# The first half's mixers as steps between the in-projections' products, in place of a ranked plan, with their loads and stores on GpSimd's queue

## The chip, the core and the metric

The kernel runs on one core of one Trainium2 chip. The metric is device time in microseconds of one execution; less is better. A core has five engines with queues of their own, each worked off strictly in order: PE (TensorE, matrix products), DVE (VectorE), ACT (ScalarE), POOL (GpSimd) and SP (SyncE, used here only to issue transfers). Transfers run on 16 DMA engines.

## The reference, cut to what matters

One hybrid decoder layer on x of 2048 tokens by 1024 features, in fp32. Three mixers read one common projection z and feed one common output projection, and an MLP follows:

```
h = rmsnorm(x, norm1_g)
z = einsum("bsd,dc->bsc", h, w_in)          # q,k,v (384 each) | conv a,gate (256 each) | gate,x (384 each)
y_attn = attention_mixer(q, k, v)           # 6 heads in 3 dilated windows, ALiBi
y_conv = silu(layernorm(conv31(a * sigmoid(gate))))
y_lru  = gelu(gate) * rg_lru(conv4(x))      # a scan along the sequence
x = x + concat(y_attn, y_conv, y_lru) @ w_out
x = x + square(relu(rmsnorm(x, norm2_g) @ w_up)) @ w_down
return rmsnorm(x, final_g)
```

## The kernel before, in words

**Tiles.** Everything lies transposed, 128 features on the partitions and tokens along the free axis. The sequence is worked in two halves h = 0, 1 of 1024 tokens. Each fp32 operand is split into two parts (`split`, L242 to L246: ACT rounds the value, DVE takes the difference), and each product is three matmuls (`products`, L262, L265, L268). The weights of a group come through `load_w` (L251 load on SP's queue, L242 on ACT, L243 on DVE), with five landing tiles (`raw`) and four pairs of split weights (`rounded6` and its neighbours), so that loads and splits run at most a few products ahead of PE.

**In-projection.** `inproj(h)` (L324) takes the groups of z's columns in the order of `COLUMN_ORDER`. For h = 0 these are [11, 9, 12] together, then [10], [0], [3], V, [1], [4], [2], [5], [16], [13], [17], [14], and [18, 15] together; for h = 1 all stand alone but the last pair, and V comes late. A one-tile group holds two PSUM banks of 512 tokens and 8 rounds of products: 48 matmuls of 128x512. `evac` (L390, L393) multiplies the finished banks by the norm's factor on DVE, and stores z to DRAM. V (`project_v`, L410) is computed with the tokens on the partitions: twice 4 banks, each time 8 weight tiles of 128x384 and 96 matmuls, 192 in all; DVE splits the 16 weight tiles (L243) and empties the 8 banks (L433). There are four main banks, so V uses all of them. Ahead of h = 1 stand its activations: 16 loads of `xt`, split on ACT (L245) and DVE (L246) with the sum of squares (L276, L277), and after its first group the norm (L286, L287 on PE, L361 on ACT, two reciprocals L362 on DVE).

**Mixers.** `mixers(0)` is a chain of generator steps: attention, then the 31-tap convolution (62 operations of 128x1024 on DVE, L472 and L474) with its layer norm, then the LRU (three tiles: a load of `lscr`, 4 taps L557 and L561, gate products L573 to L575 with ACT's sigmoids, a scan on DVE L591), then `combine` of attention. `conv_ahead(HS)` computes 31 of the second half's taps. Each `yield` names the step's cost on DVE in us.

**What sets the order.** The program is recorded in the order of the code, and a list scheduler then orders each engine's queue. In this kernel `inproj(0)` is recorded whole; ACT is told to issue two DRAM-to-DRAM copies of 4 MB each (`out_w`, `down_w`) behind its last instruction of `inproj(0)`; `setup()` (LRU gate weights and zeros, 17 small loads and stores) is placed behind the last load of x. Then `mixers(0)` is recorded as one block at a low rank (`high_priority(offset=-1500)`), and `conv_ahead(HS)` likewise inside `inproj(1)`: the scheduler fits their instructions into both in-projections wherever its ranking finds room. The first half's convolution, LRU and `combine` load and store on SP's queue, attention loads on POOL's. The second half's mixers already run in another manner, by `tick`:

```
    def tick(share):
        chore()
        credit[0] = min(credit[0] + share, 2.0 * share)
        if aside[0] is None or credit[0] <= 0:
            return
        ...
        cost = next(aside[0], None)
        ...
            credit[0] -= cost
```

Each call adds a share of credit and records at most one step, which is then bound to stand behind the products recorded so far on PE, DVE and ACT.

Of the kernel before, what the change touches and what calls it, by code (L numbers as in the profile page):

```python
# [15 lines left out]
HS = 1024  # L16
# [23 lines left out]
OUT_SHARE, UP_SHARE, DOWN_SHARE = 0.7, 1.0, 1.0  # L40
# [39 lines left out]
def body(tc, xt, w_in, w_v, w_out, w_up, w_down, vecs, lru_wa, lru_wx, consts, g_row, out, out_rows):  # L80
# [45 lines left out]
    def z_tile():  # L126
        return zp.tile([P, HS], F32, name="z", tag="Z")
# [175 lines left out]
    def project(src, group, acts, nk, evac, hook=None):  # L303
        banks = [[main_bank() if i < 2 else mix_bank() for _ in range(2)] for i in range(len(group))]
        w = {}
        if not len(acts):
            acts.between = lambda: w.update({0: load_w(src(group[0], 0))})
        for k in range(nk):
            while len(acts) < k + 1:
                acts.more()  # L310
            if hook is not None and k == hook[0]:
                hook[1]()
            for i, t in enumerate(group):
                if k % 4 == 0 and (k or i not in w):
                    w[i] = load_w(src(t, k // 4))
                products(banks[i], w[i], k % 4, acts[k], k == 0, k == nk - 1)
            while len(acts) < (min(k + 2, nk) if k < 4 else nk):
                acts.more()
        for i, t in enumerate(group):
            evac(t, banks[i])  # L320
# [3 lines left out]
    def inproj(h, after=None):  # L324
# [44 lines left out]
        def evac(t, banks):  # L369
            z = z_tile()  # L370
            for b, bank in enumerate(banks):
# [37 lines left out]
        def project_v():  # L409
# [8 lines left out]
            for c0 in range(0, HS // P, 4):  # L418
                banks = [main_bank()[:, :VW] for _ in range(4)]
                for k in range(KT):  # L420
                    wh, wl = load_w(w_v[k])
                    ah, al = acts[k]
                    for i, bank in enumerate(banks):
                        c = slice((c0 + i) * P, (c0 + i + 1) * P)
                        nc.tensor.matmul(bank, ah[:, c], wh, start=k == 0, stop=False)
                        nc.tensor.matmul(bank, ah[:, c], wl, start=False, stop=False)
                        nc.tensor.matmul(bank, al[:, c], wh, start=False, stop=k == KT - 1)
                for i, bank in enumerate(banks):
# [7 lines left out]
        for n, grp in enumerate(cols_):  # L436
            if grp[0] < 0:
                project_v()
                continue
            if after is not None:  # L440
                after(n)
# [11 lines left out]
    def loads(h):  # L453
        return nc.gpsimd if h else nc.sync

    def stores(h):
        return nc.gpsimd if h else nc.sync

    def conv_taps(t0, n, early, tiles=(0, 1)):
# [6 lines left out]
        yield 0  # L466
        yield 0
# [11 lines left out]
    def conv_norm(t0, yc, early):  # L479
        tile_, q = wide_tile if early else mtile, nc.sync if early else nc.gpsimd  # L480
# [39 lines left out]
    def conv_ahead(t0):  # L520
        a, = yield from conv_taps(t0, HS, True, (0,))
        nc.sync.dma_start(cscr, a)
# [13 lines left out]
    def lru_mixer(h):  # L536
# [6 lines left out]
        for t0 in range(h * HS, (h + 1) * HS, n):  # L543
            for t in range(3):
# [9 lines left out]
                if h:  # L554
                    yield 0
                    yield 0
# [7 lines left out]
                for c in range(0, n, NB):  # L564
# [3 lines left out]
                    yield 0  # L568
# [90 lines left out]
    def attention(h):  # L659
# [18 lines left out]
        yield 0  # L678
        yield 0
# [50 lines left out]
        for n, (g, bt, half) in enumerate(sets):  # L730
            for uu in range(2):
# [35 lines left out]
                if uu == 0 and n + 1 < len(sets):  # L767
                    got = fetch_keys(h, *sets[n + 1])
# [105 lines left out]
    def mixers(h):  # L874
# [5 lines left out]
        else:  # L880
            yield from attention(0)
            yield from conv_whole(0, HS, True)
            yield from lru_mixer(0)
            yield from combine(0)

# [720 lines left out]
    inproj(0)  # L1606
# [3 lines left out]
    with tc.issue_after(last_x[0].ins):  # L1610
        setup()
    with tc.high_priority(offset=-1500):
        run(mixers(0))
# [7 lines left out]
    def between(n):  # L1621
        if n == 4:
            with tc.high_priority(offset=-1000):
                run(conv_ahead(HS))
        elif n == len(COLUMN_ORDER[1]) - 2:
# [112 lines left out]
```

## Time and profile before

| what | value |
|---|---|
| median of 3 runs | 1988.07 us (1987.36 to 1990.78) |
| the profiled execution, its own time | 1988.35 us |
| its span in the trace | 1986.5 us |
| mean granted TensorE clock | 0.994 |
| PE busy | 1938.7 us (98% of the span), 8906 matmuls |
| DVE busy | 1448.0 us (73%) |
| ACT busy | 1054.4 us (53%) |
| POOL busy | 168.2 us (8%) |

The span is the time from the first to the last recorded instruction; 1.85 us of the execution lie outside it. `inproj(0)` fills the first 257 us, `inproj(1)` the next 250. "Busy" counts instructions that compute; an engine that waits at the head of its queue counts as idle. PEclk is the share of full speed that TensorE's clock was granted.

### The profile page before, as it was taken

The page shows a single profiled execution, that of the slowest core. Times are in us where ns is not written, and L with a number is a line of the kernel's source. Part 1 is how long each engine was busy: PE and PEld are TensorE (multiplying, and loading weights), DVE is VectorE, ACT ScalarE, POOL GpSimd, SP SyncE. Part 2 cuts the span into 40 slices and gives each one's busy share as a digit, 9 for nine tenths or more (in the row PEclk, how much of TensorE's full clock was granted, in tenths as well). Part 3 has the DMA queues.
Part 4 walks back from the last instruction along what each step waited for, and adds up shares of the span by engine and source line. Part 5 has one row for each costly group of instructions (what it writes and reads, how often), then busy time and mean ns, then how long its engine had stood idle before and what let it go on. Part 6 is the DMA issues. An engine that isn't in the chain of part 4 may idle for free.

```text
span 1986.5 us, 25512 instructions
## 1 busy us (share of the span) xinstructions
PE 1938.7 (98%) x8906; PEld 1590.3 (80%) x8906; DVE 1448.0 (73%) x1976; ACT 1054.4 (53%) x1637; POOL 168.2 (8%) x297
## 2 busy tenths in 40 slices
PE   7999979999999999999999999999999999999998
PEld 6887757779787787888888888788888887888886
DVE  7899766784568665878878899867555555577884
ACT  6145946513558764555565566346555545444343
POOL 0024100000023413000000000100000000000001
PEclk9999989999999999999999999999999999999999
DMA  5556586635556647445788687764444447786773
GB/s 170 159 160 184 161 281 200 208 125 160 184 173 185 207 149 234 169 151 179 272 292 293 225 287 248 249 194 146 149 148 149 154 148 259 240 285 212 264 260 138
DMA packets 202124, 399.78 MB, mean 201 GB/s; under 512 B 25382, under 2 KB 33814, under 8 KB 201932
## 3 DMA queue, kind: packets, MB, share of 16 engines
q1 hardware_dynamic: 182548, 342.02, 51.2%
q0 software_dynamic: 16096, 45.38, 7.9%
q10 hardware_dynamic: 3352, 10.76, 1.6%
q8 instruction: 70, 1.15, 0.2%
q14 instruction: 58, 0.48, 0.1%
HBM read 287.47 MB, written 119.00 MB: 205 GB/s over the span
## 4 chain that ended last, share of the span: by engine, by line
PE 70%; DVE 12%; DMA 9%; ACT 5%; issue 4%; SPq 0%; POOL 0%; DVEq 0%; ACTq 0%; POOLq 0%
PE bank L1153 9%; PE bank L1154 9%; PE bank L1155 9%; PE bank L1517 7%; PE bank L1515 7%; PE bank L1516 7%; PE mm L262 3%; PE mm L268 3%; PE mm L265 3%; PE bank L966 2%; PE bank L967 2%; PE bank L968 2%; DVE wide L474 2%; DMA second<-in_w_down 2%; DVE rounded L926 1%
## 5 line engine op out<-in xcount | busy, mean ns | idle before, releaser
L1153 PE MATMUL bank<-rounded,pair 128*128 128x512 f32 x896 | 351.2, 392 | 2.7 <-ACT low L1162 2.0
L1154 PE MATMUL bank<-rounded,pair 128*128 128x512 f32 x896 | 351.0, 392 | 0.0
L1155 PE MATMUL bank<-rounded,pair 128*128 128x512 f32 x896 | 350.9, 392 | 0.0
L1515 PE MATMUL bank<-rounded,rounded 128*128 128x512 f32 x688 | 268.1, 390 | 1.6 <-DVE z L1528 0.8
L1517 PE MATMUL bank<-rounded,rounded 128*128 128x512 f32 x688 | 268.0, 389 | 1.4 <-DVE rounded L926 1.4
L1516 PE MATMUL bank<-rounded,rounded 128*128 128x512 f32 x688 | 267.7, 389 | 0.0
L926 DVE TENSOR_TENSOR rounded<-rounded 128x1024 fp32r<-128x1024 f32 (+1 forms) x172 | 186.9, 1098 | 73.0 <-ACT rounded L925 72.6
L925 ACT CAST rounded<-rounded 128x1024 fp32r<-128x1024 f32 (+1 forms) x172 | 161.1, 949 | 132.2 <-DMA rounded<-fscr 92.1
L1153 PEld LDWEIGHTS bank<-rounded,pair 128*128 128x128 f32 x896 | 168.4, 188 | 40.1 <-ACT low L1162 2.4
L1155 PEld LDWEIGHTS bank<-rounded,pair 128*128 128x128 f32 x896 | 168.2, 188 | 36.0 <-issue 0.2
L1154 PEld LDWEIGHTS bank<-rounded,pair 128*128 128x128 f32 x896 | 168.2, 188 | 35.4 <-issue 0.2
L262 PE MATMUL mm<-rounded,rounded 128*128 128x512 f32 x496 | 159.7, 398 | 8.5 <-ACT rounded L242 6.6
L265 PE MATMUL mm<-rounded,rounded 128*128 128x512 f32 x496 | 158.6, 396 | 0.0
L268 PE MATMUL mm<-rounded,rounded 128*128 128x512 f32 x496 | 157.8, 395 | 0.0
L925 ACT CAST rounded<-kept 128x1024 fp32r<-128x1024 f32 x80 | 84.0, 1050 | 136.8 <-DVE kept L1325 67.0
L1515 PEld LDWEIGHTS bank<-rounded,rounded 128*128 128x128 f32 x688 | 129.1, 188 | 29.5 <-DVE z L1528 1.3
L1517 PEld LDWEIGHTS bank<-rounded,rounded 128*128 128x128 f32 x688 | 129.2, 188 | 29.1 <-DVE rounded L926 2.3
L1516 PEld LDWEIGHTS bank<-rounded,rounded 128*128 128x128 f32 x688 | 129.2, 188 | 27.0
L242 ACT CAST rounded<-raw 128x512 fp32r<-128x512 f32 (+1 forms) x96 | 55.7, 583 | 145.1 <-PE mm L265 91.1
L925 ACT CAST pair<-wraw 128x1024 fp32r<-128x1024 f32 x64 | 67.1, 1048 | 112.6 <-PE bank L1154 108.3
L926 DVE TENSOR_TENSOR rounded<-kept,rounded 128x1024 fp32r<-128x1024 f32 x80 | 97.8, 1223 | 38.4 <-ACT rounded L925 38.1
L926 DVE TENSOR_TENSOR pair<-wraw,pair 128x1024 fp32r<-128x1024 f32 x64 | 78.2, 1222 | 61.6 <-ACT pair L925 61.5
(375 smaller groups left out, 3680.3 us busy)
## 6 DMA issues: line engine op xcount, KB each, us to landing
fscr<-low SPq DMA_DIRECT2D x224, 256.0 KB, 2.1
rounded<-fscr SPq DMA_DIRECT2D x112, 512.0 KB, 3.9
second<-in_w_down SPq DMA_DIRECT2D x80, 512.0 KB, 5.4
kept<-in_w_down SPq DMA_DIRECT2D x48, 512.0 KB, 5.3
raw<-in_w_in SPq DMA_DIRECT2D x64, 256.0 KB, 3.9
low<-in_w_up SPq DMA_DIRECT2D x64, 256.0 KB, 3.1
wraw<-in_w_up SPq DMA_DIRECT2D x64, 256.0 KB, 2.9
raw<-in_xt SPq DMA_DIRECT2D x32, 256.0 KB, 3.4
```

What stands on the lines that cost most here:

```text
L242: nc.scalar.copy(h, raw)
L262: nc.tensor.matmul(bank, wh[:, sl], ah[:, cols], start=first_, stop=False)
L265: nc.tensor.matmul(bank, wh[:, sl], al[:, cols], start=False, stop=False)
L268: nc.tensor.matmul(bank, wl[:, sl], ah[:, cols], start=False, stop=last_)
L925: nc.scalar.copy(h, raw)
L926: nc.vector.tensor_sub(l, raw, f32(h))
L1153: nc.tensor.matmul(bank, wh[:, sl], hi(x), start=fresh and k == 0, stop=False, **kw)
L1154: nc.tensor.matmul(bank, wh[:, sl], lo(x), start=False, stop=False, **kw)
L1155: nc.tensor.matmul(bank, wl[:, sl], hi(x), start=False, stop=k == KH - 1, **kw)
L1515: nc.tensor.matmul(banks[j], th[:, c], sh[:, x], start=fresh and k0, stop=False, **kw)
L1516: nc.tensor.matmul(banks[j], th[:, c], sl[:, x], start=False, stop=False, **kw)
L1517: nc.tensor.matmul(banks[j], tl[:, c], sh[:, x], start=False, stop=k1, **kw)
```

## The change

`mixers(0)` is no longer recorded as a block. It becomes the generator `aside[0]` at the third group of `inproj(0)`, and `tick(0.85)` is called after every `products`, `tick(1.275)` after every weight tile of V. `until` holds the chain back with steps of no cost till the column tiles it needs are recorded, and `landing` puts four such steps (two in the second half) behind each load. The order of the chain changes: convolution taps until V is recorded, then attention, then the rest of the convolution, the LRU, `combine`, and at last `conv_ahead(HS)`. What is left at the last pair of `inproj(1)` is drained there. `setup()` moves to the second group of `inproj(0)`. All loads and stores of the first half's mixers go to POOL's queue, but for the first taps' load of `uscr`. PE has the same products before and after.

```diff
+                tick(IN_SHARE)
...
+                    tick(1.5 * IN_SHARE)
...
     def loads(h):
-        return nc.gpsimd if h else nc.sync
+        return nc.gpsimd
     def stores(h):
-        return nc.gpsimd if h else nc.sync
+        return nc.gpsimd
+    def until(h, *tiles):
+        while not all((h, t) in ready for t in tiles):
+            yield 0
+    def landing(h):
+        for _ in range(2 if h else 4):
+            yield 0
...
         else:
+            conv = conv_whole(0, HS, True)
+            while (0, -1) not in ready:
+                yield next(conv)
             yield from attention(0)
-            yield from conv_whole(0, HS, True)
+            yield from conv
+            yield from until(0, *range(LG_T, LX_T + 3))
             yield from lru_mixer(0)
             yield from combine(0)
+            yield from until(1, CA_T, CG_T)
+            yield from conv_ahead(HS)
...
-    inproj(0)
+    def during_first(n):
+        if n == 1:
+            with tc.issue_after(last_x[0].ins):
+                setup()
+        elif n == 2:
+            aside[0] = mixers(0)
+    inproj(0, during_first)
     with tc.issue_after(next(i for i in reversed(nc.cur_bb.bb.instructions) if i.engine == mybir.EngineType.Activation)):
         nc.scalar.dma_start(out_w, w_out)
         nc.scalar.dma_start(down_w, w_down[0:2 * KT, :, 0:NB])
-    with tc.issue_after(last_x[0].ins):
-        setup()
-    with tc.high_priority(offset=-1500):
-        run(mixers(0))
...
-        if n == 4:
-            with tc.high_priority(offset=-1000):
-                run(conv_ahead(HS))
-        elif n == len(COLUMN_ORDER[1]) - 2:
+        if n == len(COLUMN_ORDER[1]) - 2:
+            while aside[0] is not None:
+                tick(1e9)
+            credit[0] = 0.0
             close("wide")
```

**First place: DVE at the beginning of V in `inproj(0)`.** Before, from the second evacuation of column tile 3 on (`z_599`; `wide_2250` and `wide_2253` are the convolution's two running sums, `rounded6_83` are parts of V's weights):

```order
L390 TENSOR_TENSOR z_599<-mm_544,row1_105 128x512
L243 TENSOR_TENSOR rounded6_83<-raw2_101,rounded6_83 128x384
L474 SCALAR_TENSOR_TENSOR wide_2250<-wide_2248,vec_130,wide_2250 128x1024
L474 SCALAR_TENSOR_TENSOR wide_2253<-wide_2251,vec_130,wide_2253 128x1024
L243 TENSOR_TENSOR rounded6_83<-raw3_102,rounded6_83 128x384
L474 SCALAR_TENSOR_TENSOR wide_2250<-wide_2248,vec_130,wide_2250 128x1024
```

Now, from the same evacuation (`z_682`; the running sums are `wide_557` and `wide_560`):

```order
L394 TENSOR_TENSOR z_682<-mm_617,row1_105 128x512
L486 SCALAR_TENSOR_TENSOR wide_560<-wide_558,vec_130,wide_560 128x1024
L486 SCALAR_TENSOR_TENSOR wide_557<-wide_555,vec_130,wide_557 128x1024
L486 SCALAR_TENSOR_TENSOR wide_560<-wide_558,vec_130,wide_560 128x1024
L486 SCALAR_TENSOR_TENSOR wide_557<-wide_555,vec_130,wide_557 128x1024
L486 SCALAR_TENSOR_TENSOR wide_560<-wide_558,vec_130,wide_560 128x1024
L486 SCALAR_TENSOR_TENSOR wide_557<-wide_555,vec_130,wide_557 128x1024
L486 SCALAR_TENSOR_TENSOR wide_560<-wide_558,vec_130,wide_560 128x1024
L243 TENSOR_TENSOR rounded6_83<-raw1_100,rounded6_83 128x384
L486 SCALAR_TENSOR_TENSOR wide_560<-wide_558,vec_130,wide_560 128x1024
L243 TENSOR_TENSOR rounded6_83<-raw2_101,rounded6_83 128x384
```

Seven taps stand ahead of the first weights of V that follow the evacuation, and from the first evacuation row to V's last weights there are 30 taps in the row, where attention's work was mixed in before.

**Second place: ACT at the end of `inproj(0)`.** Before: the last activations of the second half (L245, L276), the cast of its first weights, then attention's casts, and the gelu of the last column tile with the two copies behind it:

```order
L245 ACTIVATE rounded1_78<-raw0_99,vec_130 128x512
L276 ACTIVATE tmp0_96<-raw0_99 128x512
L242 CAST rounded6_83<-raw1_100 128x512
...
L404 ACT_TABLE_LOAD
L404 ACTIVATE z_1475<-z_1475 128x1024
L1608 DMA out_w_124<-in_w_out 64x16384
L1609 DMA down_w_126<-in_w_down 2048x512
```

Now the same piece:

```order
L408 ACTIVATE z_2307<-z_2307 128x1024
L1631 DMA out_w_124<-in_w_out 64x16384
L1632 DMA down_w_126<-in_w_down 2048x512
L276 ACTIVATE tmp1_97<-raw0_99 128x512
L276 ACTIVATE tmp2_98<-raw1_100 128x512
L245 ACTIVATE rounded1_78<-raw2_101,vec_130 128x512
...
L276 ACTIVATE tmp0_96<-raw0_99 128x512
L242 CAST rounded6_83<-raw1_100 128x512
```

The gelu, which waits for the last evacuation, and the two copies now stand ahead of the last ten operations of the second half's activations and of the cast of its first weights.

**Third place: SP at the same time.** Before, the last stores of `inproj(0)` (`lscr` and `gscr` from z), with weights of the second half's first groups ahead of them and the LRU's first load between them:

```order
L251 DMA raw1_100<-in_w_in 128x512
L251 DMA raw2_101<-in_w_in 128x512
L542 DMA wr_2372<-gates_w_123 128x512 x2
L407 DMA lscr_111<-z_1471 128x1024
L251 DMA raw3_102<-in_w_in 128x512
L251 DMA raw4_103<-in_w_in 128x512
L550 DMA wide_2375<-lscr_111 128x1027
L405 DMA gscr_112<-z_1475 128x1024
```

Now:

```order
L411 DMA lscr_111<-z_2303 128x1024
L339 DMA raw2_101<-in_xt 128x512
L339 DMA raw3_102<-in_xt 128x512
L409 DMA gscr_112<-z_2307 128x1024
L339 DMA raw4_103<-in_xt 128x512
L339 DMA raw0_99<-in_xt 128x512
L251 DMA raw1_100<-in_w_in 128x512
L251 DMA raw2_101<-in_w_in 128x512
```

The LRU's load is gone from here, and the second half's last four loads of x and all its weights stand behind the store of `lscr`; two loads of x and the weights stand behind the store of `gscr`, which waits for the gelu.

More of the change, by code (lines that the diff above doesn't have):

```diff
@@ L39 @@
 A11, A12, A22, S1, S2, S3, S4, A21 = range(8)
-OUT_SHARE, UP_SHARE, DOWN_SHARE = 0.7, 1.0, 1.0
+IN_SHARE, OUT_SHARE, UP_SHARE, DOWN_SHARE = 0.85, 0.7, 1.0, 1.0
 T_AT = ((2, 3), (16, 17), (8, 9), (10, 11), (12, 13), (14, 15))
@@ L322, in body, with inproj @@
     last_x = [None]
-    def inproj(h, after=None):
+    ready = set()
+    def inproj(h, after):
         sq = row_tile()
@@ L370, in evac @@
             z = z_tile()
+            ready.add((h, t))
             for b, bank in enumerate(banks):
@@ L436, in inproj @@
         for n, grp in enumerate(cols_):
+            after(n)
             if grp[0] < 0:
                 project_v()
+                ready.add((h, -1))
                 continue
-            if after is not None:
-                after(n)
             src = lambda t, q: w_in[t if t < V_T else t - 3][:, q * NB:(q + 1) * NB]
@@ L465, in conv_taps @@
             ys.append(tile_()[:, :n])
-        yield 0
-        yield 0
+        yield from landing(0 if early else 1)
         for k in range(TAPS):
@@ L479, in conv_norm @@
     def conv_norm(t0, yc, early):
-        tile_, q = wide_tile if early else mtile, nc.sync if early else nc.gpsimd
+        tile_, q = wide_tile if early else mtile, nc.gpsimd
         s = tile_()[:, :NB]
@@ L521, in conv_ahead @@
         a, = yield from conv_taps(t0, HS, True, (0,))
-        nc.sync.dma_start(cscr, a)
+        nc.gpsimd.dma_start(cscr, a)
     def conv_rest(t0):
@@ L553, in lru_mixer @@
                 u = work(h)[:, :n]
-                if h:
-                    yield 0
-                    yield 0
+                yield from landing(h)
                 nc.vector.tensor_scalar(u, x[:, 0:n], v("lru_conv_w", t * LTAPS), v("lru_conv_b", t), op0=OP.mult, op1=OP.add)
@@ L567, in lru_mixer @@
                     yield 0.7
-                    yield 0
+                    yield from landing(1)
                     for m, (dst, name) in enumerate(((r, "lru_ba"), (i, "lru_bx"))):
@@ L677, in attention @@
         got = fetch_keys(h, *sets[0])
-        yield 0
-        yield 0
+        yield from landing(h)
         qs, keys, vv, lead = split_keys(*got)
@@ L767, in attention @@
                 if uu == 0 and n + 1 < len(sets):
+                    yield from until(h, Q_T + sets[n + 1][0], K_T + sets[n + 1][0])
                     got = fetch_keys(h, *sets[n + 1])
```

## The prediction

> **What bounds the kernel now.** I read the page first: it says which engine sets the end.
>
> ```profile
> span 1986.5 us, 25512 instructions
> PE 1938.7 (98%) x8906; PEld 1590.3 (80%) x8906; DVE 1448.0 (73%) x1976; ACT 1054.4 (53%) x1637; POOL 168.2 (8%) x297
> PE   7999979999999999999999999999999999999998
> ```
>
> PE is busy for 98% of the span, and the change leaves its products alone. So at most 1986.5 − 1938.7 = 48 us of idle PE can be won in the whole kernel, and little of it where the row of tenths shows a 9; the two 7s and the 8 stand at the start, near 250 to 300 us and at the end. Next I read stretches of the in-projections, engine by engine.
>
> ```profile
> core 0: us, PE busy (x) PEld busy (x) DVE busy (x) ACT busy (x) POOL busy (x), PEclk, DMA share, GB/s
> 80.00:118.00 38.00, 37.98 (x229) 36.71 (x229) 37.38 (x62) 15.24 (x35) 9.27 (x16) 1.00 0.70 199
> 118.00:158.00 40.00, 39.79 (x214) 32.17 (x213) 39.55 (x65) 16.46 (x43) 11.61 (x19) 1.00 0.45 138
> 222.00:257.00 35.00, 34.66 (x163) 27.85 (x161) 27.52 (x52) 34.28 (x68) 0.00 (x0) 1.00 0.59 182
> 277.00:301.00 24.00, 10.67 (x30) 8.14 (x29) 18.31 (x17) 4.01 (x6) 0.00 (x0) 0.66 0.77 248
> ```
>
> In V's stretch (80 to 118 us) and behind it DVE is full to 38 and 40 us, and PE still is not held up: the ranked plan put as much of the mixers there as fits. One stretch is broken: from 277 to 301 us PE works 10.67 of 24 us, at 0.66 of its clock. The waits of PE over the first 450 us name the reason, and the chain of what ended last its origin.
>
> ```profile
> PE cb L573 <- ACT wr L242: 11.6, 2, 10.1
> PE mb L753 <- DVE stat L755: 3.7, 2, 3.3
> PE mm L425 <- DVE z L393: 2.5, 1, 2.5
> ...
> PE cb L574 <- DVE state L593: 1.2, 1, 1.2
> ...
> 260.31 21.47 DMA wide<-lscr
> 281.80 0.82 DVE wide L557
> 282.64 1.29 DVE wide L561
> 286.57 3.32 DVE row L362 x2
> ```
>
> The LRU's first gate product (L573) stands in PE's queue ahead of ready in-projection work; it waits for taps that wait 21.47 us for one load of 0.5 MB, and PE stands 10.1 us. Behind it a reciprocal and attention cost another 3.3 us. The load is slow because of the two 4 MB copies: of the transfers from 260 to 272 us, and from 272 to 282 us, the trace says
>
> ```profile
> q10 hardware_dynamic: 61, 4.00, 99.8%
> q1 hardware_dynamic: 101, 0.25, 5.4%
> ...
> q10 hardware_dynamic: 623, 1.43, 44.3%
> q1 hardware_dynamic: 514, 1.43, 43.5%
> ```
>
> (packets, MB, share of the engines). For 12 us ACT's copies (q10) take all, SP's queue (q1) gets 0.25 MB; then they share, and q1 moves 0.143 MB per us.
>
> **The change, part by part.** The sum is made against the profiled execution, 1988.35 us, which is 0.28 us above the median of the three runs, 1988.07.
>
> *1. What the stall was worth.* A matmul of 128x512 takes 0.228 us of PE at full clock and nearly twice that after the stall:
>
> ```profile
> 274.60 0.62 PE L265 MATMUL mm<-rounded,rounded 128*128 128x512 f32 x2
> 275.05 0.62 PE L268 MATMUL mm<-rounded,rounded 128*128 128x512 f32 x2
> ...
> 288.35 1.05 PE L265 MATMUL mm<-rounded,rounded 128*128 128x512 f32 x2
> 289.20 1.05 PE L268 MATMUL mm<-rounded,rounded 128*128 128x512 f32 x2
> ...
> 291.65 0.62 PE L268 MATMUL mm<-rounded,rounded 128*128 128x512 f32 x2
> ```
>
> (0.45 us from pair to pair, then 0.85, and at 291.65 the old length again). The 30 matmuls from 277 to 301 us are worth at most 30 × 0.228 = 6.8 us, so at least 17.2 of the 24 us are lost there; since some of the 30 are smaller products, I take 18. The LRU's load now comes long after the copies: −18.
>
> *2. What comes late next.* The order shows (second and third place) that the second half's last activations and its first weights, which before were ready at 256 us, now stand behind the last evacuation, the gelu and both copies' issue, and their loads behind the store of `gscr`. Let T be PE's last product of `inproj(0)`. The four evacuations, the gelu, and a split of weights behind the load take
>
> ```profile
> 256.22 2.48 DVE L393 TENSOR_TENSOR z<-mm,row 128x512 f32<-128x512 f32 x4
> 257.60 1.28 ACT L404 ACT_TABLE_LOAD   x1
> 258.90 1.06 ACT L404 ACTIVATE z<-z 128x1024 f32<-128x1024 f32 x1
> ```
>
> 2.5 + 1.1 = 3.6 us (the table loads while the evacuations run), then the copies start and the SP queue's next transfers with them: 0.5 MB of `gscr`, two loads of x and the first weights, 0.25 MB each, 1.25 MB in all. By the rows above the first 12 us bring 0.25 MB, the other 1.0 MB at 0.143 MB per us takes 7.0 us; rounding and splitting the weights adds 1.3 us. The weights are ready at T + 3.6 + 19 + 1.3 = T + 24. PE has nothing else: all its other steps stand behind the same products. After the pause of before PE ran at half clock to about 291 us, 4 us after its first product, so 2 us are lost to that again; and the norm's square root and two reciprocals (L362, 3.32 us on the chain above) hold the second group some 2 us. Together 28, against 18 removed: **+10**. If the loads escape the copies, transfers land as the trace's DMA issues do where they are undisturbed:
>
> ```profile
> raw<-in_w_in SPq DMA_DIRECT2D x13, 256.0 KB, 3.0
> ...
> wide<-gscr SPq DMA_DIRECT2D x1, 512.0 KB, 5.7
> ```
>
> Then the weights are ready at T + 3.6 + 3.0 (x) + 1 + 3.0 + 1.3, about 12 us, and with the norm's 2 us the net is −4; −6 if the two loads behind `gscr` overlap in full. If q1 starves for the whole 21.47 us that the LRU's load took and then moves its 1.0 MB, the weights come at T + 33 and the upper end is +19.
>
> The 12 us of starvation are one observation. The Trainium skill, "DMA: Bandwidth & Descriptors", section "SWDGE vs HWDGE vs iDMA", says that each DMA engine goes round-robin between the queues that feed it; taken as even shares, that rule would give the loads their part from the start and make the sum 10 us less (rival b). The trace disagrees with even shares: 99.8% against 5.4% of the engines, with 64 KB in each of q10's 61 packets and 2.5 KB in each of q1's 101.
>
> *3. V in `inproj(0)` becomes DVE's.* DVE's queue holds, from the evacuation of column tile 3 to V's last weights, 30 taps, 16 splits of weights and (between V's halves) the 4 evacuations of its first four banks; PE has 192 matmuls.
>
> ```profile
> 73.47 6.06 DVE L474 SCALAR_TENSOR_TENSOR wide<-wide,vec 128x1024 f32<-128x1024 f32 x5
> 95.14 2.19 DVE L433 TENSOR_SCALAR z<-mm,rcol 128x384 f32<-128x384 f32 x4
> 97.25 1.02 DVE L243 TENSOR_TENSOR rounded<-raw,rounded 128x384 fp32r<-128x384 f32 x2
> ...
> 103.72 0.33 PE L426 MATMUL mm<-rounded,rounded 128*128 128x384 f32 x1
> ...
> 106.84 0.34 PE L426 MATMUL mm<-rounded,rounded 128*128 128x384 f32 x1
> ```
>
> One tap takes 1.20 us (five in 6.06 us, with the tail of the last), four evacuations 2.2, a split 0.5; from the first to the last of these PE rows 18 matmuls take 3.12 us, 0.173 each. So PE needs 192 × 0.173 = 33.3 us, DVE 36.0 + 8.0 + 2.2 = 46.2, and with V's last evacuations, for which the next groups' banks wait, another 2.2: 48.4. Since all four main banks are V's, PE can do nothing else but the mixers' own products, and attention has not begun. The order leaves DVE no way to take weights ahead of taps. Loss 48.4 − 33.3 = 15, against about 1 in this stretch before (PE busy 37.98 of 38): **+14**. The lower end is +8, if weights split before the evacuation cover the first seven taps (7 × 1.2 = 8.4, less the 2 us that one weight tile gives PE); the upper +18, if the waits come at each of 16 tiles as a round trip over ACT's rounding (0.5 us) too.
>
> *4. Attention moves away from the taps.* Between [1] and [14] DVE no longer has taps. Where before it was full (39.55 of 40) PE still idled 0.2 us; the stretch to 257 us idles 0.3. What could be won is hidden in stretched small products: **−2** (−6 to +1).
>
> *5. The start.* `setup()`'s 17 transfers now stand ahead of the weights of the second and third group on SP's queue, and four of them wait for casts. Before, loads of weights were mixed among them. The splits of these weights come later by that, behind the first group's norm, where PE waits already:
>
> ```profile
> 35.83 0.50 PE L286 MATMUL mb<-rounded,ones_cr 128*128 128x512 f32 x1 [1.41 <-ACT rounded L242]
> ...
> 46.74 0.50 PE L262 MATMUL mm<-rounded,rounded 128*128 128x512 f32 x1 [0.48 <-DVE z L393]
> ```
>
> **+2.5** (0, if those weights still land before 46 us, to 4, one landing of 3.0 us and a split).
>
> *6. The rest of `inproj(1)`.* Before, PE waited 1.2 us at a gate product and 2.5 us at V for DVE; now LRU and `combine` run there with one bank for gates (six gate products that wait for a sigmoid, up to 1 us each) and on POOL's queue, where a load stands behind the stores recorded ahead of it: **−1** (−6 to +6). At the beginning of the out-projection the first weights' split now stands behind the last evacuations (2.48 us, row above): **+2** (0 to +4).
>
> Sum: 10 + 14 − 2 + 2.5 − 1 + 2 = +25.5, that is 1988.35 + 25.5 = 2014 us. The ends add up to −6 + 8 − 6 + 0 − 6 + 0 = −10 and 19 + 18 + 1 + 4 + 6 + 4 = +52.
>
> **The rivals.**
> (a) *The stall goes and nothing takes its place* (faster). Price: the loads of x and weights get through ahead of the copies, −6; V +8 by the weights split ahead; −6, 0, −6 and 0 for the rest: −10, 1978 us. It decides at whether the xt loads land before ACT reaches the copies. For it: the gelu is only some 3.6 us behind T, and a load takes 3.0 to 3.9 us. Against: two loads stand behind `gscr` on SP, which waits for that gelu. Chance 0.17.
> (b) *The queues share evenly*: from the copies' start q1 moves 0.143 MB per us, as it did from 272 to 282 us. Then 1.25 MB take 9 us and not 19, term 2 is 0 and the time 2004 us. For it: the later row. Against: the 12 us before. Chance 0.10; if V costs only 8 besides and terms 5 and 6 nothing, about +4, 1992 us: 0.10.
> (c) *Full starvation and slow clock*: q1 starves for 21 us, +19, V +18, the rest +8: +45, 2033 us. The 21.47 us for one load speak for it. Chance 0.18.
> (d) *The plan does not bind*: the scheduler moves mixers ahead anyway. The order shows it doesn't: seven taps stand ahead of V's weights. Chance 0.02, with no change.
>
> **How the numbers follow.** My forecast, with a DVE-bound V and late weights, has 0.43; its own range is 2003 to 2025. Less than 0.2% (4 us) can't be told from no change on this kernel. Faster by more takes (a), 0.17, and a little of (b): 0.18. Within it lie (d) and half of (b)'s lower case: 0.08. Slower: 0.74. The range holds the forecast, (b), (c) to 2035 and the upper edge of (a): 1981 to 2035.
>
> **What would show it.** Right: in the changed trace PE idles in many pieces of 0.3 to 1.5 us in V with the release "DVE rounded L243", about 14 us in all; one gap of 20 us or more lies before the first product of `inproj(1)`, released by ACT or DVE splits of `raw` behind a load of x or w, with q1 near nothing beside q10; L573 shows no gap of 10 us. Wrong: V's stretch stays at 34 us, or the first product of `inproj(1)` follows T within 12 us (rival a), or new waits of PE for the LRU or `combine` lie behind POOL's queue (term 6).

## The result and the profile after

The changed kernel takes 2012.4 us in the median of four runs (2010.42 to 2013.27), the kernel before 1988.02 us in four. The ratio is 1.0119, with a 95% interval of 1.0101 to 1.0136: slower by 24 us. The profiled execution took 2012.82 us, with a span of 2010.7 us and a granted clock of 0.988. Its page says where to look:

```profile
span 2010.7 us, 25503 instructions
PE 1942.2 (97%) x8906; PEld 1594.0 (79%) x8906; DVE 1449.6 (72%) x1976; ACT 1049.7 (52%) x1632; POOL 203.6 (10%) x360
PE   8999949999999999999999999999999999999998
```

PE has the same 8906 matmuls, and its busy time is up by 3.5 us, with a granted clock of 0.988 in place of 0.994. DVE has the same 1976 operations. What is new is a 4 in the row of tenths, in the slice from 251 to 302 us, where a 7 stood before: the worst place is the same, and worse. The waits of PE over the two in-projections (0 to 560 us) name three places:

```profile
PE mm L262 <- ACT rounded L242: 33.9, 2, 26.9
PE mm L430 <- DVE rounded L243: 6.3, 4, 4.8
PE mm L429 <- DVE z L438: 2.5, 2, 1.3
PE mm L429 <- ACT rounded L242: 2.3, 1, 2.3
PE mm L262 <- DVE z L397: 2.1, 1, 2.1
```

(The other 7.0 us of the first row are the wait for the first weights of all, 6.6 before.) The 26.9 us stand ahead of the first product of the second half. The gate products that waited 10.1 us before (L573) are not among the waits any more. V waits for splits of its weights on DVE (L430 is the second of V's three products).

The same stages in both kernels, as the end of the last matmul of each group in PE's timeline. (In the kernel after, the last two matmuls of [10] run behind the first four of [3] and end at 60.87 us; the row gives the end of the matmul that makes up the same count of 192 from the start.)

| end of | before, us | after, us | difference |
|---|---|---|---|
| [10] | 57.90 | 59.96 | +2.1 |
| [3] | 79.66 | 81.72 | +2.1 |
| V, first half | 117.14 | 129.11 | +12.0 |
| [14] | 234.37 | 249.11 | +14.7 |
| [18, 15], first half | 256.65 | 274.20 | +17.6 |
| [9], second half | 302.95 | 330.05 | +27.1 |
| [17], second half | 437.45 | 459.59 | +22.1 |
| V, second half | 475.51 | 499.20 | +23.7 |
| [18, 15], second half | 508.19 | 532.11 | +23.9 |
| the span | 1986.5 | 2010.7 | +24.2 |

V's stretch, by engine, in windows of 25 us (busy us and counts, then PEclk, DMA share and GB/s):

```profile
75.00:100.00 25.00, 20.19 (x97) 18.32 (x96) 25.00 (x25) 3.27 (x8) 2.40 (x4) 0.93 0.23 74
100.00:125.00 25.00, 22.52 (x110) 20.08 (x109) 25.00 (x30) 5.77 (x11) 4.77 (x8) 0.93 0.51 150
275.00:300.00 25.00, 0.00 (x0) 0.00 (x0) 10.93 (x18) 8.85 (x13) 0.00 (x0) 0.53 0.94 331
```

DVE has no idle time at all from 75 to 125 us; that is what a bound engine looks like, and PE beside it is at 20 and 22 of 25. From 275 to 300 us nothing runs on PE, and the DMA engines are 94% busy. The chain of what ended last, and the queues and landings of issues from 274 to 287 us, tell of that stretch:

```profile
280.61 19.77 DMA raw<-in_w_in
...
301.07 1.22 PE mm L262 x2
```

```profile
q10 hardware_dynamic: 50, 3.28, 64.7%
q1 hardware_dynamic: 361, 0.91, 26.5%
...
raw<-in_xt SPq DMA_DIRECT2D x4, 256.0 KB, 16.9
...
gscr<-z SPq DMA_DIRECT2D x1, 512.0 KB, 17.5
raw<-in_w_in SPq DMA_DIRECT2D x2, 256.0 KB, 19.8
```

The load that waits beside the two copies is now the second half's first weights, 19.8 us for 0.25 MB, where it was the LRU's input, 21.5 us, before.

### The profile page after: what moved, and what is told of

It is laid out like the page before. It is cut to its first block, busy times and chain, and to the rows that moved or that the text cites. A ratio compares the mean times of both kernels' runs of the same rounds, so it can differ in the third digit from the quotient of the medians.

```text
span 2010.7 us, 25503 instructions
## 1 busy us (share of the span) xinstructions
PE 1942.2 (97%) x8906; PEld 1594.0 (79%) x8906; DVE 1449.6 (72%) x1976; ACT 1049.7 (52%) x1632; POOL 203.6 (10%) x360
## 4 chain that ended last, share of the span: by engine, by line
PE 77%; DVE 9%; DMA 6%; ACT 4%; issue 3%; SPq 0%; POOL 0%; DVEq 0%; ACTq 0%
PE bank L1169 9%; PE bank L1170 9%; PE bank L1171 9%; PE bank L1533 7%; PE bank L1531 7%; PE bank L1532 7%; PE mm L262 5%; PE mm L265 5%; PE mm L268 5%; DVE wide L486 2%; PE bank L984 2%; PE bank L983 2%; PE bank L982 2%; DVE rounded L942 2%; DMA rounded<-fscr 1%
## 5 line engine op out<-in xcount | busy, mean ns | idle before, releaser
L1532 PEld LDWEIGHTS bank<-rounded,rounded 128*128 128x128 f32 x688 | 129.2, 188 | 26.9
L1531 PEld LDWEIGHTS bank<-rounded,rounded 128*128 128x128 f32 x688 | 129.1, 188 | 26.9 <-issue 0.2
L262 PEld LDWEIGHTS mm<-rounded,rounded 128*128 128x128 f32 x496 | 92.7, 191 | 60.3 <-ACT rounded L242 36.8
```

The lines of the kernel that those rows point to most:

```text
L262: nc.tensor.matmul(bank, wh[:, sl], ah[:, cols], start=first_, stop=False)
L1531: nc.tensor.matmul(banks[j], th[:, c], sh[:, x], start=fresh and k0, stop=False, **kw)
L1532: nc.tensor.matmul(banks[j], th[:, c], sl[:, x], start=False, stop=False, **kw)
```

## The experiments

The time of a run is the median of its runs; "before" was run beside each group of kernels on the same chip (medians 1988.5 to 1989.7 us). Since single executions of one kernel differ by several us, a claim on a stage rests on the profiled execution's timeline, and a claim on the time on the median.

**1. Rows of 2 KB in the first copy** (label e1_rows2k).

```diff
-        nc.scalar.dma_start(out_w, w_out)
+        for c in range(2):
+            nc.scalar.dma_start(out_w[:, :, c * NB:(c + 1) * NB], w_out[:, :, c * NB:(c + 1) * NB])
```

> The changed kernel, with the first of the two copies (out_w, 4 MB) written as two copies with rows of 2 KB in place of one with 64 rows of 64 KB; the order on every engine stays. Theory (the first loads of inproj(1) starve behind the 64 KB packets of that copy): SP's queue gets its part from the copies' start, the gap of 26.9 us ahead of the first product of inproj(1) falls to 14 to 19 us, the time by 8 to 13 us, to about 2002. Rival (the loads come late because they stand behind the gelu and the store of gscr on SP, whatever the copies do): the gap stays within 3 us of 26.9 and the time at 2010 to 2014. Second rival (the bytes of both copies take the DMA engines, whatever their packets): the gap falls by less than 5 us.

Measured: 2012.19 us (2009.03 to 2019.22), no change; the gap ahead of `inproj(1)` is 23.6 us. The chain, ACT's timeline, and the queues and issues from 278 to 290 us:

```profile
290.14 9.87 DMA raw<-in_w_in
```

```profile
279.61 9.31 ACTq L1633 DMA_DIRECT2D down_w<-in_w_down  x1
...
288.96 1.15 ACT L276 ACTIVATE tmp<-raw 128x512 f32<-128x512 f32 x2 [7.63 <-issue]
```

```profile
q10 hardware_dynamic: 1020, 2.07, 56.3%
q1 hardware_dynamic: 606, 1.55, 36.4%
...
raw<-in_xt SPq DMA_DIRECT2D x4, 256.0 KB, 9.6
```

The packets did what was expected of them: SP's queue gets its part from the start, and a load of weights takes 9.9 us, not 19.8. But the first weights are issued at 290.1 us, not at 280.6, so that the gap shrinks by 3.3 us only. The reason stands in ACT's timeline (an ACTq row is the issue of a transfer by ACT). Behind the re-cut first copy, ACT's issue of the second one lasted 9.31 us; in the changed kernel it lasted 0.60. Its gelu done, ACT stood still for 7.63 us, and the squares (L276) that read the last tiles of x, and so free a `raw` tile for the weights, came only from 288.96 us on. The edit thus changed two things at once: the queue's share and ACT's time. The gap is as small a step from 26.9 us as the second rival named, but not for the rival's reason, and what even shares alone are worth is not shown. The time is no clean measure either: the profiled execution is the slowest of the four, 2019.22 us, and ends the second in-projection when the changed kernel does (532.25 and 532.11 us).

**2. The copies later** (e2_late): both copies issued at the fourth group of `inproj(1)`.

```diff
+        if n == 3:
+            with tc.issue_after(next(i for i in reversed(nc.cur_bb.bb.instructions) if i.engine == mybir.EngineType.Activation)):
+                nc.scalar.dma_start(out_w, w_out)
+                nc.scalar.dma_start(down_w, w_down[0:2 * KT, :, 0:NB])
```

> The changed kernel, with both copies issued at the fourth group of inproj(1) in place of its beginning. Theory (starvation by the copies): the first product of inproj(1) comes 10 to 13 us after the last one of inproj(0) (evacuation 2.6, gelu with table 2.3, a load of x 3, a load of weights 3, rounding 1.3), 14 us less than now; part of it, 0 to 8 us, comes back where the copies now run, as a wait for weights or for a load on GpSimd's queue; the time falls by 6 to 14 us, to about 2002. Rival (the order of the loads alone): the gap stays at 24 us or more.

Measured: 2003.59 us (2002.35 to 2010.83), about 9 us less. PE's timeline at that place, and two landings from 270 to 300 us:

```profile
286.52 1.22 PE L262 MATMUL mm<-rounded,rounded 128*128 128x512 f32 x2 [11.56 <-ACT rounded L242]
```

```profile
raw<-in_w_in SPq DMA_DIRECT2D x10, 256.0 KB, 2.9
raw<-in_xt SPq DMA_DIRECT2D x6, 256.0 KB, 3.8
```

So of the 26.9 us, 15.3 come from the copies beside the loads and 11.6 from the order (the last evacuation, the gelu, a load of x and one of weights in a row). Of the 15.3 some 4 came back by the end of `inproj(1)` in small waits at gate products behind the moved copies; [18, 15] of the second half ended 10.2 us earlier.

**3. Half the taps in V** (e3_v_half).

```diff
-                    tick(1.5 * IN_SHARE)
+                    tick(0.75 * IN_SHARE if h == 0 else 1.5 * IN_SHARE)
```

> The changed kernel, with half the credit in the first half's V, so that 16 fewer of the 30 taps stand between V's weights there; they come after attention. Theory (V is bound by DVE, at 1.20 us for each tap): V takes 35 to 38 us in place of 47.3, and the end of V comes 10 us earlier. The taps come back in the last groups of inproj(0) and in the first of inproj(1): if PE hides them there the time falls by 8 to 11 us, to 2001 to 2004; if the activations of the second half get later by them, by less. Rival (V waits for the loads or the rounding of its weights on ACT, or for DVE's evacuations): V stays above 43 us.

Measured: V takes 37.8 us in place of 47.3 and ends 9.4 us earlier, as the theory had it; but the time is 2015.13 us (2013.05 to 2018.78), not lower. The second in-projection ends 8.8 us earlier, and the out-projection gives it back:

```profile
PE bank L984 <- DVE pair L942: 6.9, 1, 6.9
PE bank L984 <- DVE rounded L942: 2.8, 1, 2.8
...
535.70 1.20 DVE wide L486
```

The tap steps that V did not take pushed the whole chain back, and the second half's taps ran into the drain, ahead of the splits of the out-projection's weights. V is bound by DVE, and the work isn't free where it lands.

**4. The first half's loads and stores back on SP's queue** (e4_sp_queue).

```diff
     def loads(h):
-        return nc.gpsimd
+        return nc.gpsimd if h else nc.sync
```

and the same for `stores`, for the stores behind `conv_norm` and for `cscr`.

> The changed kernel, with the loads and stores of the first half's convolution, LRU and combine back on SP's queue; the steps stay. Theory (the queue is not what costs the 24 us): the time stays within 4 us of 2012, the gap ahead of inproj(1) at 24 to 28 us and V at 47 us. Rival (waits behind the stores on GpSimd's queue cost time in LRU and combine): the time falls by 4 us or more, in inproj(1). Second rival (the change of queue protects SP's weight loads): the time rises by 4 us or more, as waits for weights in inproj(1).

Measured: 2008.71 us (2007.34 to 2013.11), 3.7 us below the changed kernel's median: just within the 4 us that the theory allows. The first gap is 27.5 us and the first V 47.5 us: no difference there. In the changed kernel's second V DVE waits 5.8 us for a load of `combine` that stands on POOL's queue, and PE waits 2.3 us for V's weights and 1.2 for an evacuation:

```profile
DVE m L862 <- DMA m<-oscr: 5.8, 1, 5.8
...
PE mm L429 <- ACT rounded L242: 2.3, 1, 2.3
PE mm L429 <- DVE z L438: 1.2, 1, 1.2
```

On SP's queue that V takes 34.1 us in place of 39.5, and no such wait is left (0.2 us of PE between 455 and 505 us). So the queue costs some 3 to 5 us, late in `inproj(1)`, whose last matmul ends 4.1 us earlier in this run. Which of these waits makes it up isn't separated: PE's 2.3 us are a wait for weights whose load took 8.03 us on the chain of the changed kernel, and not for `combine`. The two intervals of the ratios, 1.0084 to 1.0116 and 1.0101 to 1.0136, overlap, so the total alone doesn't settle it.

**5. The kernel before, with the re-cut copy** (e5_before_rows2k), the edit of the first run.

> The kernel before, with out_w copied in rows of 2 KB as in the first run of this call. Theory (the 21.5 us of the LRU's load came from the 64 KB packets): the load takes 8 to 12 us, the wait of 10.05 us at the gate product falls to 0 to 3, and the time by 6 to 14 us, to about 1978. Rival (the bytes of the copies count): the load still takes 17 us or more, and the time stays within 4 us of 1988.

Measured: 1982.79 us (1980.87 to 1991.15), ratio 0.9979 (0.9963 to 0.9994). The LRU's load takes 10.9 us, [9] ends 12.1 us earlier than before. But waits of 3.5 us and, at the next gate product, of 7.9 us appear, and [17] ends only 1.3 us earlier:

```profile
wide<-lscr SPq DMA_DIRECT2D x1, 513.5 KB, 10.9
...
261.87 11.08 ACTq L1610 DMA_DIRECT2D down_w<-in_w_down  x1
...
314.98 0.80 PE L574 MATMUL cb<-wr 128*128 128x512 f32 x1 [7.94 <-DVE wr L243]
```

The wait of 10 us at L573 went, as expected (one of 2.6 us is left there, at 366 us, where one of 1.6 was before); a wait at L574, behind small loads of attention beside the copies, took its place. As in run 1, the re-cut first copy made the issue of the second one long: it held ACT for 11.08 us, and the wait of 3.5 us, of the first product behind the norm for ACT's root (L361), follows from that. So here too the gain is one of shorter loads less one of a held ACT.

**6. The kernel before, with late copies** (e6_before_late): both at the ninth group of `inproj(1)`, as in run 2.

> The kernel before, with both copies issued at the ninth group of inproj(1) in place of its beginning. Theory (the copies cost the kernel before its stall of some 18 us): the LRU's load takes 4 to 6 us, the waits of 10 and 3.3 us between 277 and 301 us go, [11] and [9] of the second half take together 24 to 30 us in place of 45, and the time falls by 8 to 18 us, to 1970 to 1980. Rival (the LRU's gate product is late without the copies too, by DVE's order): a wait of 7 us or more stays at the gate products and the time falls by less than 6 us.

Measured: 1984.97 us (1982.24 to 1992.95), ratio 0.9982 (0.9971 to 0.9994). The LRU's first load takes 7.0 us, the waits of 10 and 3.3 us are gone, [11] and [9] take 32 us from the first product to the end, a little more than the 24 to 30 expected. And yet [18, 15] of the second half ends only 1.8 us earlier. PE waits 7.1 us at V, because DVE is full ahead of it:

```profile
340.00:390.00 50.00, 46.49 (x202) 37.29 (x201) 14.06 (x20) 11.66 (x16) 2.10 (x4) 1.00 0.89 301
390.00:440.00 50.00, 39.58 (x167) 31.51 (x165) 49.57 (x51) 10.13 (x15) 0.00 (x0) 0.93 0.29 94
...
PE mm L425 <- DVE z L393: 7.1, 1, 7.1
...
360.76 1.66 ACT L242 CAST rounded<-raw 128x512 fp32r<-128x512 f32 x3 [17.23 <-DMA mscr<-m]
```

DVE, 49.57 of 50 us busy with the second half's taps, was at 36.78 and 49.43 in the same windows of the kernel before. Here it is at 14.06 while the copies run, and then too late. The last line says what went with that: ACT issued the first copy at 342.92 us and the second only at 360.21, and did nothing for 17.23 us between, a pause that the trace puts down to another transfer (`mscr`) beside the first copy. So re-cutting or moving the copies won 3 to 6 us of the time, and not the 18 that the stall looked like; but each of the two edits also held ACT, for 11 and 17 us, and what they would win without that was not tried.

**7. Three edits at once** (e7_late_spread): late copies, fewer taps in V, and a credit of 1.1.

> The changed kernel with three edits at once: copies at the fourth group of inproj(1), V of the first half with half the taps, and a credit of 1.1 in place of 0.85 at the other products, so that the taps taken out of V are not left to the end of inproj(1). Theory (24 us = taps in V and loads beside the copies; with half the taps alone they came back as a full DVE at the end of inproj(1)): V takes 38 us, the gap ahead of inproj(1) 11 to 14, no wait over 3 us at the start of the out-projection, and the time falls to 1990 to 1997. Rival (DVE's work returns wherever it is put): the time stays at 2000 or more, with waits of PE for DVE in the attention stretch or in inproj(1).

Measured: 2008.37 us (2007.35 to 2011.06). The rival holds. With 1.1 the taps pile up in DVE's queue already in [0] and [3], because a step of two taps has a declared cost of 1.5 and takes 2.4 us, V takes 43.2 us against the 38 expected, and early in it PE waits once for long for its weights:

```profile
PE mm L430 <- DVE rounded L243: 7.2, 1, 7.2
```

The gap ahead of `inproj(1)` is 16.2 us without a copy beside it, where 11 to 14 were expected, and gate products wait 0.8 to 1.7 us seven times.

**8. `setup()` one group later** (e8_setup_later).

> The changed kernel, with setup() recorded one group later, so that weights of the second group stand ahead of its transfers on SP's queue again. Theory of the prediction (the transfers delay those weights): the second group [10] starts without the wait of 2.1 us and takes 11.2 us in place of 13.4, the time falls by about 2 us. Rival (PE waits for the norm's reciprocals, which end at the same time in both kernels; it came there 1.8 us earlier, so that the pause is in one piece, and the clock falls by it): the wait of 2.1 us and the 13.4 us of [10] stay.

Measured: [10] starts without the wait and takes 11.06 us, and [3] ends at 78.68 us, 3.0 us earlier than in the changed kernel: the theory of the prediction holds for the stage. The in-projections end 3.2 us earlier. The time is 2013.08 us (2012.72 to 2015.12) all the same; in the profiled execution the 3 us are lost again in small pieces between 660 and 1730 us, which the edit doesn't touch. That part stays open.

**9. The taps between attention's steps** (e9_woven): half the credit in V as in run 3, and

```diff
+    def woven(main_, side):
+        for n, cost in enumerate(main_):
+            yield cost
+            if n % 4 == 3:
+                more = next(side, None)
+                if more is not None:
+                    yield more
...
-            yield from attention(0)
+            yield from woven(attention(0), conv)
             yield from conv
```

with a credit of 1.05 behind V.

> The changed kernel with half the taps in V, as in the run that halved V's credit, and the taps left over put between attention's steps, one tap step after each fourth of them, at a credit of 1.05 from there on. Theory (the taps cost nothing where DVE has room, and attention's stretch has it: DVE was busy 13 to 14 of 25 us there): V takes 35 to 38 us, attention's stretch no more than before by 3 us, no wait over 3 us at the start of the out-projection; the copies still starve the loads, so that a gap of 15 to 27 us stays ahead of inproj(1); the time falls by 6 to 14 us, to 1998 to 2006. Rival (DVE's work returns wherever it is put, because the steps stand in DVE's queue ahead of evacuations and weights): the attention stretch grows by what V wins and the time stays at 2008 to 2016.

Measured: 1997.18 us (1993.43 to 2000.99), ratio to before 1.0035 (1.0021 to 1.0048): 15 us below the changed kernel. V takes 37.8 us, no tap is left behind attention, and the first half's last group ends at 271.7 us, 2.5 us earlier than in the changed kernel. The gap ahead of `inproj(1)` is 5.8 us, and it is no load of weights that ends it:

```profile
PE mm L262 <- DVE z L397: 7.6, 4, 4.4
PE mm L262 <- ACT rounded L242: 6.8, 1, 6.8
PE mm L262 <- DVE rounded L246: 5.8, 1, 5.8
```

In the changed kernel, a row of eight taps still ran then, and the first split of the second half's activations (L246) began behind it, at 266.26 us:

```profile
256.70 9.65 DVE L486 SCALAR_TENSOR_TENSOR wide<-wide,vec 128x1024 f32<-128x1024 f32 x8
```

Without a row of taps ahead of them, the second half's activations and the loads behind them run while PE still works on the first half: in the timeline SP issues the first weights at 268.02 us, and ACT the copies at 277.21 us. So most of the 26.9 us hang on the place of the taps, by way of the activations and the copies that come after. The run changed the credit in V, the weaving and the credit of 1.05 together; the credit in V alone (run 3) left a gap of 25.1 us, so it isn't that one. Attention's stretch, [1] to [14], takes 125.8 us from V's end, 5.8 us more than in the changed kernel, so DVE's room there isn't quite free.

**10 and 11. All edits together** (e10_all: run 9, late copies as in run 2, `setup()` as in run 8, SP's queue as in run 4; e11_all_copies9: the same with the copies at the tenth group).

> The woven kernel of this call, and also: copies at the fourth group of inproj(1), setup() one group later, and the first half's loads and stores on SP's queue. Theory: the single effects add up: 10 us for the copies, 2 to 3 for setup(), 3 for the queue below the woven kernel's time, 1984 to 1992, near the kernel before or below it. Rival (waits of DVE move on to the next place, as in the kernel before when its copies were moved): 1995 or more.

> The kernel of the last run, with the copies issued at the tenth group of inproj(1) in place of the fourth, when the LRU's loads are through. Theory (there the copies met the LRU's load, 12 us, and PE waited 8.4 us at a gate product as in the kernel before): that wait goes, [1] of the second half takes 12 to 14 us in place of 24.9, and the time falls by 6 to 12 us, to 1985 to 1991. Rival (the wait moves on, to the loads of combine or the weights of V beside the copies, or to a DVE that is full with the second half's taps): [1] gets shorter, but V or the start of the out-projection gets longer, and the time stays at 1993 or more.

Measured: 1997.18 us (1994.53 to 2004.53) and 1994.47 us (1990.69 to 2000.28). The effects do not add up. In the first, the copies meet the store of `uscr` and the LRU's load, and a gate product waits as in the kernel before; its chain and its wait:

```profile
328.87 11.84 DMA uscr<-z
340.77 12.06 DMA wide<-lscr
...
PE cb L583 <- ACT wr L242: 8.4, 1, 8.4
```

In the second this wait is gone, [1] takes 13.3 us, as expected; but the next thing beside the copies is late, a wait of 7.5 us for weights, and one of 7.3 us on the chain for the load of V's weights:

```profile
PE mm L262 <- ACT rounded L242: 19.6, 3, 7.5
PE mm L429 <- ACT rounded L242: 3.3, 1, 3.3
...
419.55 1.14 ACT L242 CAST rounded<-raw 128x512 fp32r<-128x512 f32 x2 [25.97 <-DMA m<-wscr]
```

The last line shows where the 7.5 us come from: the rounding of those weights waited on ACT's queue. As in run 6, ACT issued the second copy long after the first, here at 419.00 us, 28 us later, and stood still for 25.97 us ahead of it, in wait for another transfer (`m<-wscr`) that came in behind the first copy. In run 10 the same pause lasted 13.08 us.

**12. The kernel before with the copies in pieces** (e12_before_pieces): eight pieces of 0.5 MB of each copy, at eight groups.

> The kernel before, with both copies cut into eight pieces of 0.5 MB each, one of each copy issued at each of the fourth to the eleventh group of inproj(1). Theory (the copies cost by their collision with other loads, and in pieces of 1 MB per 11 us none starves for long): no wait over 3 us between 257 and 440 us, and the time at or below that of the kernels with moved or re-cut copies, 1978 to 1985. Rival (DVE is full behind, so that time won ahead of it is lost at V): [9] ends some 12 us earlier than before, but V gets longer and the time stays within 4 us of 1984.

Measured: 2010.69 us (2008.01 to 2012.47): the time fits neither theory. [17] ends 4.4 us earlier than before and no wait over 2.1 us is left between 280 and 440 us. But the first product of the out-projection that needs a later pair waits

```profile
PE bank L966 <- ACT pair L925: 18.3, 1, 18.3
...
500.00:530.00 30.00, 17.07 (x74) 13.36 (x72) 28.21 (x28) 3.78 (x5) 0.00 (x0) 0.83 0.16 53
```

with DVE 28.21 of 30 us busy, 21.8 of them with 17 taps, while it was busy for 11.96 of 40 us from 360 to 400 us. The pieces, each tied to the last ACT instruction recorded, seem to have changed how the ranked plan placed the second half's taps. Why the scheduler put them late was not tried.

## Why the prediction was right, point by point

**The time.** Forecast 2014 us, measured 2012.4; forecast +25.5 us on the profiled execution, measured 2012.82 − 1988.35 = +24.5. The two large causes, late weights and a V bound by DVE, were the right ones. That the total came out to 1 us is in part luck: V fell short of its term by 4.1 us and attention exceeded its own by 7.6, and the other terms missed by 0.4 to 2.2 us each, all downward.

Two slips of the working change nothing in the forecast. The lower case of rival (b), V at +8 and terms 5 and 6 at nothing, adds up to 0 + 8 − 2 = +6, and not to +4. And V's upper end by a round trip at each of 16 tiles would be 14 + 8 = +22, and not +18.

**The stall that goes and the one that comes (term 2, +10).** Right in size: from T to the end of [9] the difference grows from +17.6 to +27.1, +9.5. The wait at L573 went; the first product came 26.9 us after T, against the 24 that the sum gave (3.6 + 19 + 1.3). ACT issued the copies at 275.75 us, 3 us before the gelu's end, and not behind it, and a load took 19.8 us. Its cause was right too, the copies beside the loads (run 2: 11.6 us without them, forecast 12), and the order as the other part.

Starvation by the large packets, as the term had it, shows too. From 281 to 288 us ACT's queue (q10) moved 2.82 MB and SP's (q1) 0.07; from 291 to 300 us they moved 1.56 and 1.68 MB. With rows of 2 KB in the first copy, loads took 9.9 and 10.9 us (runs 1 and 5) in place of 19.8 and 21.5. What even shares would be worth in time, 10 us by rival (b), stays open: the edit that made the shares nearly even also held ACT for 9.3 and 11.1 us.

The Trainium skill, "DMA: Bandwidth & Descriptors", section "SWDGE vs HWDGE vs iDMA", has the engines go round-robin between the queues. Run 1 comes nearer to even shares, with packets of more like size (1020 of 2.07 MB in all and 606 of 1.55 MB): 56.3% to 36.4% of the engines. Whether SP's queue always had a packet ready there isn't shown.

**The −18.** The stall of the kernel before was read rightly as a wait for one load (runs 5 and 6: [9] ends 12 us earlier without it), but its worth in time isn't shown to be 18: runs 5 and 6 win 3 to 6 us, since in run 5 the next gate product waits and ACT is held, and in run 6 ACT stands still and DVE is full some 100 us later. In the changed kernel part of the loss comes back soon: between [9] and [17] of the second half the difference falls from +27.1 to +22.1, as PE waited 3.1 us at gate products there before and doesn't now, and has 569 products there in place of 575. Term 6, a net of such things, was forecast at −1 and measured −3.2 to the end of `inproj(1)`.

**V (term 3, +14).** DVE's 48.4 us were right: 47.3 measured. Mis-sized is what it was set against: the step took 34 us for V before, and the table shows 37.4, since products of attention already ran inside V. The difference is +9.9. DVE is the reason (no idle time for 50 us; run 3: 37.8 us with 16 taps between V's weights, where there were 30). The sign that the prediction named came out in part: PE's waits add up to 7.8 us of the 47.4, and not to 14, and they are one of 4.8 us and a few of 0.5 to 1.3, not many pieces. The rest of V's lost time is a clock at half speed, twice.

**Attention (term 4, −2).** Wrong in sign. The products of attention that left V came to the later groups: V's window holds 195 products in place of 227 (192 are V's own), [1] to [14] 664 in place of 631, and [18, 15] 124 in place of 100. [1] to [14] lost 2.8 us, [18, 15] another 2.8. Terms 3 and 4 together were forecast at +12 and measured at 17.6 − 2.1 = +15.5.

**The start (term 5, +2.5).** +2.1, by the cause given (run 8).

**The out-projection's start (+2)** came to +0.3 by the end of the span; the wait for the first pair there is 0.9 us. Read nearer to that place, at the 3300th matmul (703.4 us before, 729.2 after), it is +1.8, part of which comes back later.

**The queue.** Term 6 named loads behind stores on POOL's queue; run 4 shows 3 to 5 us of it at the second V. Rival (a) needed the loads of x to land ahead of the copies. Run 9 did that, by moving taps away, and the time fell by 15 us: its point of decision was the right one.

**No better version.** Of all, the kernel before with the re-cut copy has the lowest median, 1982.79 us, ratio 0.9979 (0.9963 to 0.9994); the best with steps is 1994.47 us, still above the kernel before.

## What to carry to other kernels

When PE is busy for 98% and another engine for 70%, the question of a new order is where the other engine's work stands in its own queue, ahead of which evacuation or weight split, and not how much there is of it: a burst of 30 taps cost 10 us in V, and half of them moved in between attention's steps gave 15 us, by way of what then came earlier. A large copy that nobody waits for is best read by what loads are due while it runs, and by the engine that issues it: re-cutting or moving it held ACT for 9.3, 11.1, 13.1, 17.2 and 26.0 us in runs 1, 5, 10, 6 and 11. Moving it away from one load only pays if what comes next has time to spare; run 2, where ACT wasn't held, won 9 us. A stall's length is not its worth: follow the next stage to where another engine becomes the bound, and count what is left there.

## What the runs showed of the hardware that was not expected

- After the pause of 26.9 us PE ran at half clock for 6 us, from 301.07 to about 307.2 us (pairs 0.85 us apart, then 0.47), against 4 us after the 10 us pause of before:

```profile
302.09 1.05 PE L265 MATMUL mm<-rounded,rounded 128*128 128x512 f32 x2
...
307.21 0.64 PE L265 MATMUL mm<-rounded,rounded 128*128 128x512 f32 x2
```

The Trainium skill, "TensorE: Matmul & The Clock Gate", section "Part 1: The HAM clock gate", lets the full rate return after at least one busy window of about 3.4 us of sustained work. The 6 us here are more than one such window.

- ACT's queue issued the two copies at 275.75 and 276.42 us, while the gelu recorded ahead of them ran from 277.77 us: an issue did not wait for that operation to be done.

```profile
275.75 0.64 ACTq L1631 DMA_DIRECT2D out_w<-in_w_out  x1
276.42 0.60 ACTq L1632 DMA_DIRECT2D down_w<-in_w_down  x1
276.48 1.28 ACT L408 ACT_TABLE_LOAD   x1
277.77 1.06 ACT L408 ACTIVATE z<-z 128x1024 f32<-128x1024 f32 x1
```

- Inside V the granted clock fell to half twice, which makes the mean of 0.93 from 75 to 125 us. The first time it stood behind PE's wait of 4.81 us (0.50 from 93 to 95 us); the second time (0.64, 0.50, 0.50 and 0.66 in the four windows of 1 us from 109 to 113 us) no wait of PE since 92 us had been longer than 1.33 us.

- How long an issue holds ACT depended on what stood in the queue ahead of it. Behind one copy with rows of 64 KB, the second copy's issue took 0.60 us (the changed kernel); behind the same bytes as two copies with rows of 2 KB, it took 9.31 and 11.08 us (runs 1 and 5).
